# An encoder layer: two column blocks by feature half behind each sublayer, and another place for three small pieces of work

## The chip, the core and the metric

The kernel runs on one core of one Trainium2 chip. TensorE (PE) multiplies matrices, VectorE (DVE), ScalarE (ACT) and GpSimd (POOL) work on tiles in on-chip memory, and SyncE (SP) issues the DMA transfers. The metric is the device time of one execution in microseconds (us); lower is better.

## What is computed

One layer of an encoder on 256 tokens of 2048 features, in float32:

```python
f = _swiglu(_rmsnorm(h, ffn1_pre_g[i]), ffn1_w_gate[i], ffn1_w_up[i], ffn1_w_down[i])
h = h + 0.5 * _rmsnorm(f, ffn1_post_g[i])
m = _mixer(_rmsnorm(h, mix_pre_g[i]), w_qkv[i], na_rpb[i], out_g[i], w_o[i])
h = h + _rmsnorm(m, mix_post_g[i])
f = _swiglu(_rmsnorm(h, ffn2_pre_g[i]), ffn2_w_gate[i], ffn2_w_up[i], ffn2_w_down[i])
h = h + 0.5 * _rmsnorm(f, ffn2_post_g[i])
g = jax.nn.sigmoid(_rmsnorm(h, ple_pre_g[i]) @ w_ple_gate[i])
h = h + _rmsnorm(g * (p[i] @ w_ple_proj[i]), ple_post_g[i])
```

`_swiglu(u, wg, wu, wd)` is `(silu(u @ wg) * (u @ wu)) @ wd` with 5632 hidden features; `_mixer` projects to q, k and v for 16 heads of 128 features, attends (4 heads over a two-dimensional neighbourhood, 12 over dilated windows) and projects back with `w_o`. The last step adds a small input embedding `p`. `_rmsnorm` divides by the root of the mean square over the features and multiplies by a gain.

## The kernel before

**Tiles.** Tokens form two tiles `t` of 128; features are cut into slices `k` of 128 (16 of them) and into column blocks of 512, four slices each. `h`, the residual, stays on chip, tokens on partitions. For a product the left side must lie transposed, features on partitions: `transposed_split` (L238) turns four slices of a tile by TensorE (`tr`, L242, two banks), multiplies by the row gain (`y_g`, L246) and splits the result in a rounded part `u_h` (L248, ScalarE) and the rest `u_l` (L249, VectorE).

**Products.** A float32 product is made of three products of shorter precision: `mac` (L91, L92, L93) issues wh·u_h, wh·u_l and wl·u_h for each slice. A weight tile is loaded by SP (`raw`, L65, three buffers of 1 MB), rounded by ScalarE (`wh`, L73) and subtracted by VectorE (`wl`, L74). `product` (L101) runs over the slices in steps of eight, within a step over both token tiles, and can call `mid` before the last three slices of the last step. `pair_product` (L137) makes a gate block and an up block together from fewer products, with sums of token tiles made by `token_sums` (L252 to L267: `y_s` on VectorE, `sums_h` on ScalarE, `sums_l` on VectorE). Column block 0 of each feed-forward sublayer goes through `product` instead, gate first, then up.

**Start.** `load_x` (L292) fetches x transposed, two slices at a time (`xb`), and makes `u_h` (L300) and `u_l` (L301) with the row gain. The first gate block takes 1, 1, 2, 2, ... slices a step, so that work starts early. x·gain for the token sums is L373; the sums follow in the text of the program, and then the up block, four slices a step.

**Behind each sublayer.** The last down blocks are added to `f` (L401), their squares summed by ScalarE (`sq`, L235), and `f` multiplied by the gain in place (L404). `rsqrt_mean` (L223) makes the token's factor: a reduce on VectorE (L228) and two steps on POOL (L229, L230). `residual` (L320) then computes `h` (L332) block by block, and transposes it for the next sublayer. It is a generator, advanced at `mid` and after it, the first two column blocks of both tiles ahead of the last two. The next product starts as soon as the first `u_h` is there.

**Order.** The program is written for a framework that fixes the order of instructions on each engine when it is built, by its own estimates, and takes buffers from pools in turn. Each engine works through its own list in order; an instruction that waits holds all behind it on that engine.

Of the kernel before, what the change touches and what calls it, by code (L numbers as in the profile page):

```python
# [15 lines left out]
P = 128  # L16
# [17 lines left out]
def encoder_layer(ctx: ExitStack, tc: tile.TileContext, a: dict, out: bass.AP):  # L34
# [21 lines left out]
    make_identity(nc, ident)  # L56
    mhalf = const.tile([P, 16], F32, name="mhalf")
    nc.gpsimd.memset(mhalf, -0.5)


    def load_rows(w, r0, n, c0, pool=wpool, bufs=3):
# [39 lines left out]
    def product(  # L101
        acc, lhs, w, r0, c0, first=True, last=True, steps=None, ahead=None, mid=None, jobs=True
    ):

        nk = len(lhs)
        s0 = 0
        for n in steps or [nk % SUPER] * (nk % SUPER > 0) + [SUPER] * (nk // SUPER):
            if ahead is not None:
                ahead(s0)
            parts = load_parts(w, r0 + s0 * P, n, c0)
            for t in range(NT):
                xs = of_tile(lhs[s0 : s0 + n], t)
                lead, tail = first and s0 == 0, last and s0 + n == nk
                cut = n - MID if mid is not None and t == NT - 1 and s0 + n == nk else 0  # L120
                if cut > 0:
                    mac(acc[t], xs[:cut], parts[:cut], first=lead)
                    lead = False
                if mid is not None and t == NT - 1 and s0 + n == nk:
                    mid()
                cut = max(cut, 0)
                mac(acc[t], xs[cut:], parts[cut:], first=lead, last=tail)
            s0 += n
            if jobs:
                run_later()  # L130

    def run_later():
        for job in later:
            job()
        later.clear()
# [178 lines left out]
    def prenorm_factor(t):  # L314
# [2 lines left out]
            squares(h[:, t, b * NB : (b + 1) * NB], ss[:, b : b + 1])  # L317
        return rsqrt_mean(ss, D, 1.0)

    def residual(fg, ssf, scale, blocks, rs, g, sums=None):  # L320

        blocks += [new_split(acts, "u", D // NB) for _ in range(D // NB)]
        r, y0 = [], []
        for b0 in range(0, D // NB, 2):
            for t in range(NT):
                if b0 == 0:
                    r.append(rsqrt_mean(ssf[t], D, scale))
                for b in range(b0, b0 + 2):  # L330
                    cols = slice(b * NB, (b + 1) * NB)
                    nc.vector.scalar_tensor_tensor(  # L332
                        h[:, t, cols], fg[:, t, cols], r[t], h[:, t, cols], op0=ALU.mult, op1=ALU.add
                    )
# [14 lines left out]
    def swiglu(pool, f, ssf, res, blocks, rs, sums, w_gate, w_up, w_down, g_post):  # L349
        lhs = rows(blocks)  # L350
        ffn_pool[0] = pool
        f0 = 0

        def gated(x, t):
            y = pool.tile([P, NB], F32, name="gs", bufs=3)
            nc.scalar.activation(y, x, AF.Silu, scale=rs[t])
            return y

        for gi, ng in enumerate(FF_GROUPS):
            hid = []  # L360
            for nb in range(f0, f0 + ng):
                c0 = nb * NB
                if nb > 0:
                    gate, up = pair_product(lhs, sums, w_gate, c0, w_up, c0)
                    gs = [gated(gate[t], t) for t in range(NT)]
                else:
                    gate, up = accs("gate"), accs("up")
                    if rs is None:
                        steps = [1, 1] + [2] * 7
                        product(gate, lhs, w_gate, 0, c0, steps=steps, ahead=load_x)  # L370
                        for i, x in enumerate(x_first):
                            g = row_g[:, 0, 2 * i : 2 * i + 2].unsqueeze(2).broadcast_to([P, 2, S])
                            nc.vector.tensor_tensor(x, x, g, op=ALU.mult)  # L373
                        a1, a2 = x_first
                        half = [slice(t * P, (t + 1) * P) for t in range(NT)]
                        sums += token_sums(*(x[:, :, h_] for h_ in half for x in (a1, a2)))
                        product(up, lhs, w_up, 0, c0, steps=[4] * 4, ahead=load_h)
                        rs = [prenorm_factor(t) for t in range(NT)]
                        gs = [gated(gate[t], t) for t in range(NT)]
                    else:  # L380
                        product(gate, lhs, w_gate, 0, c0)
                        gs = [gated(gate[t], t) for t in range(NT)]
                        product(up, lhs, w_up, 0, c0)
                split_ = new_split(pool, "hid", 3)
                for t in range(NT):
                    y = up[t] if nb > 0 else pool.tile([P, NB], F32, name="hm", tag="part", bufs=6)
                    nc.vector.scalar_tensor_tensor(y, up[t], rs[t], gs[t], op0=ALU.mult, op1=ALU.mult)
                    later.append(lambda y=y, s_=split_, t=t: transposed_split(y, *s_, t))
                hid.append(split_)
            last = gi == len(FF_GROUPS) - 1  # L390
            hrows = rows(hid)
            for b in range(D // NB):
                gp = gain(g_post, b * NB, "g_post") if last else None
                acc = accs("down")

                def down_out(t):
                    f_t = f[:, t, b * NB : (b + 1) * NB]
                    if gi == 0:
                        nc.scalar.copy(f_t, acc[t])
                    else:  # L400
                        nc.vector.tensor_tensor(f_t, f_t, acc[t], op=ALU.add)  # L401
                    if last:
                        squares(f_t, ssf[t][:, b : b + 1])
                        nc.vector.tensor_tensor(f_t, f_t, gp, op=ALU.mult)  # L404

                def mid():
                    down_out(0)
                    if last and b == D // NB - 1:
                        next(res)

                product(acc, hrows, w_down, f0 * NB, b * NB, steps=[KB] * ng if b == 0 else None, mid=mid)
                down_out(1)
            f0 += ng
# [16 lines left out]
    with ExitStack() as att:  # L430
# [124 lines left out]
        for g in range(4):  # L555
            if g == 0:
                c = (0, w_na, 2 * w_na)
            else:
                c = tuple(3 * w_na + i * w_dil + (g - 1) * NB for i in range(3))
            acc = accs("q")  # L560
            product(acc, lhs, a["w_qkv"], 0, c[0])
            qT = heads_transposed(acc, rq, g > 0, "qT")
            acc = accs("k")
            product(acc, lhs, a["w_qkv"], 0, c[1])
            kT = heads_transposed(acc, rs, g > 0, "kT")
            acc = accs("v")
# [80 lines left out]
    for b in range(D // NB):  # L647
        cols = slice(b * NB, (b + 1) * NB)
        gp = gain(a["ple_post_g"], b * NB, "g_post")
        acc = accs("pg")  # L650
        product(acc, lhs, a["w_ple_gate"], 0, b * NB)
        for t in range(NT):
            s = pool.tile([P, NB], F32, name="sig", bufs=2)
            nc.scalar.activation(s, acc[t], AF.Sigmoid, scale=rs[t])
            nc.vector.tensor_tensor(s, s, pp[b * NT + t], op=ALU.mult)
            squares(s, ssz[t][:, b : b + 1])
            nc.vector.tensor_tensor(z[:, t, cols], s, gp, op=ALU.mult)
# [79 lines left out]
```

## Time and profile before

| | us |
|---|---|
| three runs | 1965.56, 1967.81, 1968.16 |
| their median | 1967.81 |
| the profiled execution | 1969.06 |
| its span in the profile | 1967.0 |
| TensorE busy in it | 1941.9 |
| VectorE busy | 1340.8 |
| ScalarE busy | 994.5 |

The profiled execution is one run more, taken with a hardware profiler; its span goes from the first to the last recorded instruction. In its timeline the stages stand so: first feed-forward sublayer 0 to 722 us, mixer to 1131, second feed-forward sublayer to 1848, the input embedding's projections and gate to 1957, and the last sums and stores to 1967. Rows of a timeline give the start, the duration, engine, line, operation, output<-inputs and, in brackets, the idle time before it and what ended it. Two matmuls that follow each other directly start 0.227 us apart, although each takes 0.39: they overlap.

### The profile page before, as it was taken

To read this page: it belongs to the slowest core of one execution; us is meant where nothing else is said; L and a number is where in the kernel's file an instruction comes from. 1 tells how busy PE (TensorE), PEld (TensorE's weight loads), DVE (VectorE), ACT (ScalarE), POOL (GpSimd) and SP (SyncE) were. 2 spreads that over 40 slices of the span, in tenths; PEclk is the share of its full clock that TensorE was granted. 3 is DMA by queue.
4 is the path that set the end of the run, shared out by engine and by line. 5 is a ranking of instruction groups with operands and counts; after the bars stand their busy time and mean duration, and the time that the engine had idled before them with its cause. 6 is when DMAs were issued, how large, how long until landed. Compare 5 with 4: busy or idle time off the path is not lost.

```text
span 1967.0 us, 22833 instructions
## 1 busy us (share of the span) xinstructions
PE 1941.9 (99%) x8840; PEld 1607.5 (82%) x8840; DVE 1340.8 (68%) x1484; ACT 994.5 (51%) x1215; POOL 28.3 (1%) x47
## 2 busy tenths in 40 slices
PE   8999999999999999999999999999999999999997
PEld 6888888888888878888888878888888888888886
DVE  5874787578757776566665588747865786577764
ACT  6554555345534545544545465545543554354563
POOL 0000000000000000000000000000000000000000
PEclk9999999999999999999999999999999999999999
DMA  9665556555655556454454665655565557555563
GB/s 336 211 214 192 193 184 219 187 180 193 214 192 174 174 176 230 141 191 152 151 192 143 215 203 193 216 191 176 188 233 173 193 172 235 171 193 177 170 216 111
DMA packets 190348, 376.91 MB, mean 192 GB/s; under 512 B 6432, under 2 KB 9504, under 8 KB 189984
## 3 DMA queue, kind: packets, MB, share of 16 engines
q1 hardware_dynamic: 190240, 375.46, 56.8%
q8 instruction: 69, 1.13, 0.2%
q14 instruction: 39, 0.32, 0.0%
HBM read 373.33 MB, written 2.10 MB: 191 GB/s over the span
## 4 chain that ended last, share of the span: by engine, by line
PE 96%; DVE 2%; DMA 1%; ACT 0%; issue 0%; POOL 0%; SPq 0%; DVEq 0%; POOLq 0%; ACTq 0%
PE down L91 8%; PE down L93 8%; PE down L92 8%; PE pair_z L93 3%; PE pair_x L91 3%; PE pair_y L91 3%; PE pair_z L92 3%; PE pair_x L92 3%; PE pair_y L92 3%; PE pair_z L91 3%; PE pair_x L93 3%; PE pair_y L93 3%; PE pair_v L92 3%; PE pair_v L91 3%; PE pair_v L93 3%; PE pair_s L92 2%
## 5 line engine op out<-in xcount | busy, mean ns | idle before, releaser
L74 DVE TENSOR_TENSOR wl<-raw,wh 128x1024 fp32r<-128x1024 f32 (+1 forms) x753 | 910.4, 1220 | 447.4 <-ACT wh L73 419.1
L73 ACT CAST wh<-raw 128x1024 fp32r<-128x1024 f32 (+1 forms) x753 | 790.1, 1052 | 728.5 <-PE pair_z L92 178.5
L91 PE MATMUL down<-wh,hid_h 128*128 128x512 f32 x704 | 274.7, 391 | 0.2
L93 PE MATMUL down<-wl,hid_h 128*128 128x512 f32 x704 | 274.1, 389 | 0.0
L92 PE MATMUL down<-wh,hid_l 128*128 128x512 f32 x704 | 273.9, 389 | 0.0
L91 PEld LDWEIGHTS down<-wh,hid_h 128*128 128x128 f32 x704 | 132.2, 188 | 28.1 <-ACT hid_h L248 1.1
L93 PEld LDWEIGHTS down<-wl,hid_h 128*128 128x128 f32 x704 | 132.2, 188 | 27.4
L92 PEld LDWEIGHTS down<-wh,hid_l 128*128 128x128 f32 x704 | 132.2, 188 | 27.1
L91 PE MATMUL pair_y<-wh,u_h 128*128 128x512 f32 x280 | 108.9, 389 | 0.0
L92 PE MATMUL pair_y<-wh,u_l 128*128 128x512 f32 x280 | 108.9, 389 | 0.0
L93 PE MATMUL pair_y<-wl,u_h 128*128 128x512 f32 x280 | 108.9, 389 | 0.0
L91 PE MATMUL pair_x<-wh,u_h 128*128 128x512 f32 x280 | 108.9, 389 | 0.0
L92 PE MATMUL pair_x<-wh,u_l 128*128 128x512 f32 x280 | 108.9, 389 | 0.0
L93 PE MATMUL pair_x<-wl,u_h 128*128 128x512 f32 x280 | 108.9, 389 | 0.0
L164 DVE TENSOR_TENSOR raw<-raw 128x1024 f32<-128x1024 f32 x80 | 97.7, 1221 | 1.4
L93 PE MATMUL pair_z<-wl,u_h 128*128 128x512 f32 x240 | 93.4, 389 | 0.0
L91 PE MATMUL pair_v<-wh,u_h 128*128 128x512 f32 x240 | 93.4, 389 | 0.0
L92 PE MATMUL pair_v<-wh,u_l 128*128 128x512 f32 x240 | 93.4, 389 | 0.0
L93 PE MATMUL pair_v<-wl,u_h 128*128 128x512 f32 x240 | 93.4, 389 | 0.0
L91 PE MATMUL pair_z<-wh,u_h 128*128 128x512 f32 x240 | 93.4, 389 | 0.0
L92 PE MATMUL pair_z<-wh,u_l 128*128 128x512 f32 x240 | 93.4, 389 | 0.0
L401 DVE TENSOR_TENSOR f<-f,down 128x512 f32<-128x512 f32 x48 | 32.8, 683 | 44.4 <-PE down L93 44.4
(199 smaller groups left out, 3117.9 us busy)
## 6 DMA issues: line engine op xcount, KB each, us to landing
raw<-in_ffn_w_up SPq DMA_DIRECT2D x88, 1024.0 KB, 5.1
raw<-in_ffn_w_down SPq DMA_DIRECT2D x88, 1024.0 KB, 4.9
raw<-in_ffn_w_gate SPq DMA_DIRECT2D x84, 1024.0 KB, 5.1
raw<-in_w_qkv SPq DMA_DIRECT2D x48, 1024.0 KB, 5.1
raw<-in_w_o SPq DMA_DIRECT2D x16, 1024.0 KB, 5.0
raw<-in_w_ple_gate SPq DMA_DIRECT2D x16, 1024.0 KB, 5.2
raw<-in_ffn_w_gate SPq DMA_DIRECT2D x7, 512.0 KB, 5.7
xb<-in_xT SPq DMA_DIRECT2D x8, 256.0 KB, 5.3
```

Of the source, the lines that this page charges most:

```text
L73: nc.scalar.copy(wh[:, :n], raw)
L74: nc.vector.tensor_tensor(wl[:, :n], raw, wh[:, :n].bitcast(F32), op=ALU.subtract)
L91: nc.tensor.matmul(acc, xh, wh, start=lead, stop=False)
L92: nc.tensor.matmul(acc, xl, wh, start=False, stop=False)
L93: nc.tensor.matmul(acc, xh, wl, start=False, stop=tail)
L164: nc.vector.tensor_tensor(out_, x, y, op=ALU.add)
L401: nc.vector.tensor_tensor(f_t, f_t, acc[t], op=ALU.add)
```

## The change

Four pieces. (1) A tiny activation, `warm`, reads `mhalf` right after that is set, so the table of functions is loaded for it. (2) `halves` takes two column blocks together: the first eight slices of block a, then of block b, then the second eight of each. It is used for gate and up of the second feed-forward sublayer's first block, for q and k of the mixer's first group of heads, and for the first two gate blocks of the input embedding. (3) In the first feed-forward sublayer, the token sums are written behind the up product, and are not to be issued ahead of the latest weight load. (4) The last column block of `f`, times its gain, goes to a tile of its own, `fg`.

```diff
+    nc.scalar.activation(small.tile([P, 1], F32, name="warm"), mhalf[:, :1], AF.Copy, scale=mhalf[:, :1])
...
+    def halves(lhs, a_, b_):
+        n = len(lhs) // 2
+        for r0 in (0, n):
+            for acc, w, c0 in (a_, b_):
+                product(acc, lhs[r0 : r0 + n], w, r0 * P, c0, first=r0 == 0, last=r0 > 0)
...
+    last_f = {}
+
     def residual(fg, ssf, scale, blocks, rs, g, sums=None):
...
+                    fg_t = last_f.pop(t) if b == D // NB - 1 and t in last_f else fg[:, t, cols]
                     nc.vector.scalar_tensor_tensor(
-                        h[:, t, cols], fg[:, t, cols], r[t], h[:, t, cols], op0=ALU.mult, op1=ALU.add
+                        h[:, t, cols], fg_t, r[t], h[:, t, cols], op0=ALU.mult, op1=ALU.add
                     )
...
                         product(gate, lhs, w_gate, 0, c0, steps=steps, ahead=load_x)
-                        for i, x in enumerate(x_first):
-                            g = row_g[:, 0, 2 * i : 2 * i + 2].unsqueeze(2).broadcast_to([P, 2, S])
-                            nc.vector.tensor_tensor(x, x, g, op=ALU.mult)
-                        a1, a2 = x_first
-                        half = [slice(t * P, (t + 1) * P) for t in range(NT)]
-                        sums += token_sums(*(x[:, :, h_] for h_ in half for x in (a1, a2)))
                         product(up, lhs, w_up, 0, c0, steps=[4] * 4, ahead=load_h)
+                        with tc.issue_after(raw_loads[-1].ins):
+                            for i, x in enumerate(x_first):
+                                g = row_g[:, 0, 2 * i : 2 * i + 2].unsqueeze(2).broadcast_to([P, 2, S])
+                                nc.vector.tensor_tensor(x, x, g, op=ALU.mult)
+                            a1, a2 = x_first
+                            half = [slice(t * P, (t + 1) * P) for t in range(NT)]
+                            sums += token_sums(*(x[:, :, h_] for h_ in half for x in (a1, a2)))
...
                     else:
-                        product(gate, lhs, w_gate, 0, c0)
+                        halves(lhs, (gate, w_gate, c0), (up, w_up, c0))
                         gs = [gated(gate[t], t) for t in range(NT)]
-                        product(up, lhs, w_up, 0, c0)
...
                         squares(f_t, ssf[t][:, b : b + 1])
-                        nc.vector.tensor_tensor(f_t, f_t, gp, op=ALU.mult)
+                        fg = f_t
+                        if b == D // NB - 1:
+                            fg = last_f[t] = pool.tile([P, NB], F32, name="fg", tag="gs", bufs=3)
+                        nc.vector.tensor_tensor(fg, f_t, gp, op=ALU.mult)
...
-            acc = accs("q")
-            product(acc, lhs, a["w_qkv"], 0, c[0])
-            qT = heads_transposed(acc, rq, g > 0, "qT")
-            acc = accs("k")
-            product(acc, lhs, a["w_qkv"], 0, c[1])
-            kT = heads_transposed(acc, rs, g > 0, "kT")
+            if g == 0:
+                acc, acc_k = accs("q"), accs("k")
+                halves(lhs, (acc, a["w_qkv"], c[0]), (acc_k, a["w_qkv"], c[1]))
+                qT = heads_transposed(acc, rq, g > 0, "qT")
+                kT = heads_transposed(acc_k, rs, g > 0, "kT")
+            else:
...
-        acc = accs("pg")
-        product(acc, lhs, a["w_ple_gate"], 0, b * NB)
+        if b < 2:
+            if b == 0:
+                pg = [accs("pg"), accs("pg")]
+                halves(lhs, *((pg[i], a["w_ple_gate"], i * NB) for i in range(2)))
+            acc = pg[b]
+        else:
...
```

**At the start, on ScalarE.** The first instructions of its list before (line, operation, output<-inputs, size, and how often in a row):

```order
L300 ACT_TABLE_LOAD
L300 ACTIVATE u_h<-xb,row_g 128x256 x2
L73 CAST wh<-raw 128x512 x2
L300 ACTIVATE u_h<-xb,row_g 128x256 x2
L73 CAST wh<-raw 128x1024
L300 ACTIVATE u_h<-xb,row_g 128x256 x4
L263 CAST sums_h<-y_s 128x512
L73 CAST wh<-raw 128x1024
L263 CAST sums_h<-y_s 128x512
```

And after the change, where the line numbers of the file have grown (L75 is the cast of L73, L310 is L300, L273 is L263):

```order
L60 ACT_TABLE_LOAD
L60 ACTIVATE warm<-mhalf 128x1
L310 ACTIVATE u_h<-xb,row_g 128x256 x2
L75 CAST wh<-raw 128x512 x2
L310 ACTIVATE u_h<-xb,row_g 128x256 x2
L75 CAST wh<-raw 128x1024
L310 ACTIVATE u_h<-xb,row_g 128x256 x2
L75 CAST wh<-raw 128x1024
L310 ACTIVATE u_h<-xb,row_g 128x256 x2
L273 CAST sums_h<-y_s 128x512
L75 CAST wh<-raw 128x1024
L273 CAST sums_h<-y_s 128x512
```

The table load stands ahead of everything that needs x, and one more weight cast stands ahead of the first cast of the token sums. Both casts of the sums are still among the gate steps.

**At the start, on SP.** The transfers issued first, before:

```order
L65 DMA raw<-in_ffn_w_gate 128x512 x2
L297 DMA xb<-in_xT 128x2x256
L65 DMA raw<-in_ffn_w_gate 128x2x512
L297 DMA xb<-in_xT 128x2x256 x2
L65 DMA raw<-in_ffn_w_gate 128x4x512
L65 DMA raw<-in_ffn_w_gate 128x2x512 x2
```

and after (L67 is the weight load, L307 the load of x):

```order
L67 DMA raw<-in_ffn_w_gate 128x512 x2
L307 DMA xb<-in_xT 128x2x256
L67 DMA raw<-in_ffn_w_gate 128x2x512
L307 DMA xb<-in_xT 128x2x256
L67 DMA raw<-in_ffn_w_gate 128x2x512
L307 DMA xb<-in_xT 128x2x256
L67 DMA raw<-in_ffn_w_gate 128x2x512 x2
```

The 1 MB tile (128x4x512), gate rows for the first `pair_product`, is gone from this place; it now stands behind the fourth load of `up`. The first 1 MB load of `up` in turn now stands ahead of the last piece of x.

**Between the first feed-forward sublayer and the mixer, on VectorE.** From the last `down` block of token tile 0 (`down_5289`) on, before; `down_5290` is that of tile 1:

```order
L401 TENSOR_TENSOR f<-f,down_5289 128x512
L404 TENSOR_TENSOR f<-f,g_post 128x512
L228 TENSOR_REDUCE m<-ssf 128x1
L74 TENSOR_TENSOR wl<-raw,wh 128x1024
L332 SCALAR_TENSOR_TENSOR h<-f,r,h 128x512 x3
L246 TENSOR_TENSOR y_g<-tr,row_g 128x512 x2
L401 TENSOR_TENSOR f<-f,down_5290 128x512
L332 SCALAR_TENSOR_TENSOR h<-f,r,h 128x512
L249 TENSOR_TENSOR u_l<-y_g,u_h 128x4x128 x2
```

And after, with the same blocks named `down_5291` and `down_5292`:

```order
L414 TENSOR_TENSOR f<-f,down_5291 128x512
L420 TENSOR_TENSOR fg<-f,g_post 128x512
L238 TENSOR_REDUCE m<-ssf 128x1
L345 SCALAR_TENSOR_TENSOR h<-f,r,h 128x512 x3
L345 SCALAR_TENSOR_TENSOR h<-fg,r,h 128x512
L256 TENSOR_TENSOR y_g<-tr,row_g 128x512 x2
L76 TENSOR_TENSOR wl<-raw,wh 128x1024
L259 TENSOR_TENSOR u_l<-y_g,u_h 128x4x128 x2
L414 TENSOR_TENSOR f<-f,down_5292 128x512
```

The weight remainder `wl` moved from behind the reduce to behind `y_g`; the fourth `h` stands ahead of `y_g`, and tile 1's `f` behind `u_l`. On TensorE, in the same place, 23 instead of 15 matmuls of `q` stand ahead of tile 1's first transposes.

**Between the second feed-forward sublayer and the input embedding, on TensorE.** The projections `pp` are 48 matmuls. At their end, before:

```order
L91 MATMUL pp_14028<-wh,p_h 128x512
L92 MATMUL pp_14028<-wh,p_l 128x512
L93 MATMUL pp_14028<-wl,p_h 128x512
L242 MATMUL tr<-ident,h 128x128 x8
L91 MATMUL pg_14122<-wh,u_h 128x512
```

and after, in the middle of the 48:

```order
L93 MATMUL pp_13986<-wh,p_h 128x512
L94 MATMUL pp_13986<-wh,p_l 128x512
L95 MATMUL pp_13986<-wl,p_h 128x512
L252 MATMUL tr<-ident,h 128x128 x16
L93 MATMUL pp_14009<-wh,p_h 128x512
```

The first transposes of token tile 1 moved from behind the last `pp` matmul to the middle, with sixteen in a row where there were eight. Eight more stand behind the last `pp`, ahead of the first `pg`.

More of the change, by code (lines that the diff above doesn't have):

```diff
@@ L559, in encoder_layer @@
                 c = tuple(3 * w_na + i * w_dil + (g - 1) * NB for i in range(3))
-            acc = accs("q")
-            product(acc, lhs, a["w_qkv"], 0, c[0])
-            qT = heads_transposed(acc, rq, g > 0, "qT")
-            acc = accs("k")
-            product(acc, lhs, a["w_qkv"], 0, c[1])
-            kT = heads_transposed(acc, rs, g > 0, "kT")
+            if g == 0:
[4 more added lines that the diff above has]
+            else:
+                acc = accs("q")
+                product(acc, lhs, a["w_qkv"], 0, c[0])
+                qT = heads_transposed(acc, rq, g > 0, "qT")
+                acc = accs("k")
+                product(acc, lhs, a["w_qkv"], 0, c[1])
+                kT = heads_transposed(acc, rs, g > 0, "kT")
             acc = accs("v")
@@ L649, in encoder_layer @@
         gp = gain(a["ple_post_g"], b * NB, "g_post")
-        acc = accs("pg")
-        product(acc, lhs, a["w_ple_gate"], 0, b * NB)
+        if b < 2:
[4 more added lines that the diff above has]
+        else:
+            acc = accs("pg")
+            product(acc, lhs, a["w_ple_gate"], 0, b * NB)
         for t in range(NT):
```

## Prediction

> **What bounds the kernel now.** I read the page's share of each engine first, then its chain of work that ended last.
>
> ```profile
> PE 1941.9 (99%) x8840; PEld 1607.5 (82%) x8840; DVE 1340.8 (68%) x1484; ACT 994.5 (51%) x1215; POOL 28.3 (1%) x47
> PE 96%; DVE 2%; DMA 1%; ACT 0%; issue 0%; POOL 0%; SPq 0%; DVEq 0%; POOLq 0%; ACTq 0%
> ```
>
> TensorE is busy for 99% of the span and is 96% of the chain. The change neither adds nor removes a TensorE instruction, so only time in which TensorE stands still, or runs at half clock, can move. Next, therefore, the table of stretches (length, then busy time of PE, PEld, DVE, ACT and POOL with counts, granted clock, DMA share, GB/s).
>
> ```profile
> 0.00:40.00 40.00, 31.16 (x118) 24.57 (x119) 25.01 (x38) 24.28 (x41) 0.97 (x9) 0.96 0.90 320
> 40.00:722.00 682.00, 681.89 (x3053) 565.23 (x3053) 479.51 (x477) 342.96 (x377) 1.26 (x3) 1.00 0.59 198
> 722.00:760.00 38.00, 34.27 (x162) 26.74 (x161) 31.81 (x46) 22.45 (x41) 6.57 (x8) 1.00 0.55 182
> 1125.00:1145.00 20.00, 18.50 (x90) 14.29 (x90) 14.86 (x24) 7.88 (x13) 2.40 (x4) 1.00 0.44 152
> 1845.00:1880.00 35.00, 33.99 (x166) 27.91 (x165) 29.86 (x42) 21.35 (x35) 2.81 (x4) 1.00 0.63 218
> ```
>
> The stretches left out are as full as the second row. The idle time lies in four places, which are the four that the change touches: the start (40.00 − 31.16 = 8.8 us), the hand-off from the first feed-forward sublayer to the mixer (3.7), from the mixer to the second (1.5), and from that to the input embedding (1.0). That is 15 us in all, plus what the start loses at half clock. No change here can bring more than about 17 us, and the realistic part is smaller. The waits of TensorE say who is waited for (us in total, times, longest):
>
> ```profile
> PE gate L91 <- ACT wh L73: 8.8, 2, 7.0
> PE q L91 <- ACT u_h L248: 1.5, 1, 1.5
> PE q L93 <- DVE wl L74: 1.0, 1, 1.0
> PE gate L92 <- DVE u_l L249: 0.9, 1, 0.9
> ```
>
> **The start.** The timeline (start, duration) shows the table load first, then a stall, then the end of the first `gate` product.
>
> ```profile
> 0.86 0.11 POOL L58 MEMSET mhalf<- 128x16 f32 x1
> ...
> 4.22 1.28 ACT L300 ACT_TABLE_LOAD   x1 [4.22 <-DMA xb<-in_xT]
> 6.99 0.79 PE L91 MATMUL gate<-wh,u_h 128*128 128x512 f32 x1 [6.99 <-ACT wh L73]
> ...
> 15.04 0.62 ACT L263 CAST sums_h<-y_s 128x512 fp32r<-128x512 f32 x1 [3.00 <-DVE y_s L259]
> 15.57 1.04 ACT L73 CAST wh<-raw 128x1024 fp32r<-128x1024 f32 x1
> 16.66 0.50 PE L91 MATMUL gate<-wh,u_h 128*128 128x512 f32 x1 [1.79 <-ACT wh L73]
> ...
> 34.60 0.39 PE L92 MATMUL gate<-wh,u_l 128*128 128x512 f32 x1
> 34.83 0.39 PE L93 MATMUL gate<-wl,u_h 128*128 128x512 f32 x1
> ```
>
> The load of the function table stands behind the first piece of x, for 1.28 us. In the new order the tiny activation on `mhalf` stands ahead; `mhalf` is written at 0.86, so the load is done before x arrives. The first matmul comes at 6.99 − 1.28, about 5.7. This term, −1.3, is the surest of all.
>
> Then ScalarE waits 3.00 us for the token sums' `y_s`, with weight casts queued behind; TensorE goes idle for 1.79 us, and this is what follows, in consecutive stretches:
>
> ```profile
> 11.50:14.90 3.40, 3.37 (x15) 2.44 (x13) 3.37 (x9) 0.55 (x2) 0.00 (x0) 1.00 1.05 400
> 14.90:18.30 3.40, 1.57 (x6) 1.01 (x7) 2.88 (x5) 3.26 (x5) 0.00 (x0) 1.00 0.77 282
> 18.30:21.70 3.40, 3.40 (x10) 2.62 (x9) 3.40 (x6) 2.46 (x6) 0.00 (x0) 0.50 0.68 172
> 728.23:731.65 3.42, 1.95 (x11) 1.19 (x9) 3.42 (x7) 1.95 (x3) 0.00 (x0) 1.00 0.00 0
> 731.65:735.06 3.41, 3.09 (x14) 2.41 (x14) 2.84 (x5) 0.76 (x3) 1.53 (x2) 1.00 0.17 33
> ```
>
> A stretch of 3.40 us with TensorE busy for 1.57 (46%) is followed by one at clock 0.50, which loses half of itself, about 1.65 us. A stretch with 1.95 of 3.42 (57%) is not followed by one. The stall thus costs 1.79 + 1.65, plus small waits around it: 3.5 to 3.9 us.
>
> How much of that goes? By its words, the change writes the sums behind `up`. The built order says otherwise: the sums still stand early on VectorE and ScalarE, among the gate steps, though spread out, one weight cast and one activation further back. And the 1 MB load for the first pair of blocks, which stood on SP between the small gate loads, now stands behind the last `up` load. I follow that order by hand with the durations of the rows above (cast 1.04, sums 0.62). Without the 1 MB, at the 400 GB/s of the first of these stretches 2.6 us of transfer, the weights of the third to fifth gate steps land 2 to 3 us earlier; their casts end near 11.4, 13.9 and 16.7 instead of 16.6 and later; the wait for `y_s` falls behind a cast whose matmuls still feed TensorE. So the 1.79 and the 1.65 go. What is late next is x itself: its last piece now stands behind a 1 MB load of `up`, its `u_l` is ready near 29.4, and twelve matmuls at 0.227 (start to start, 34.60 to 34.83 as in any dense run of rows) hang on it. The last gate matmul lands near 31.5 instead of 34.83, with three `up` matmuls (0.7) already done. The start gives 34.83 − 31.5 + 0.7 = **−4.0 us**. Bounds: −1.3 if the stall stays whole, −5.2 if all goes (1.3 + 3.9).
>
> [...]
>
> **First feed-forward sublayer to mixer.** The chain from the last `down` block of token tile 0 to the first `q` matmul:
>
> ```profile
> 723.58 0.63 ACT L235 ACTIVATE sq<-f 128x512 f32<-128x512 f32 x1 [4.04 <-DVE f L401]
> 724.34 0.69 DVE L404 TENSOR_TENSOR f<-f,g_post 128x512 f32<-128x512 f32 x1 [0.85 <-ACT sq L235]
> 725.28 1.23 DVE L74 TENSOR_TENSOR wl<-raw,wh 128x1024 fp32r<-128x1024 f32 x1 [0.18 <-ACT wh L73]
> 725.46 1.45 POOL L230 TENSOR_TENSOR r<-m,mhalf 128x1 f32<-128x1 f32 x1
> 726.95 2.08 DVE L332 SCALAR_TENSOR_TENSOR h<-f,r,h 128x512 f32<-128x512 f32 x3 [0.44 <-POOL r L230]
> ...
> 730.14 0.67 DVE L401 TENSOR_TENSOR f<-f,down 128x512 f32<-128x512 f32 x1
> 731.32 0.50 PE L91 MATMUL q<-wh,u_h 128*128 128x512 f32 x1 [1.48 <-ACT u_h L248]
> 731.40 1.28 DVE L249 TENSOR_TENSOR u_l<-y_g,u_h 128x512 fp32r<-128x512 f32 x2
> 734.62 0.55 POOL L230 TENSOR_TENSOR r<-m,mhalf 128x1 f32<-128x1 f32 x1
> 735.20 2.08 DVE L332 SCALAR_TENSOR_TENSOR h<-f,r,h 128x512 f32<-128x512 f32 x3 [0.72 <-POOL r L230]
> 751.45 0.50 PE L93 MATMUL q<-wl,u_h 128*128 128x512 f32 x1 [1.00 <-DVE wl L74]
> ```
>
> What gains: `fg` doesn't overwrite what the squares read, so the multiply no longer waits 0.85 and the reduce behind it starts 0.6 earlier. No `wl` stands behind that reduce, and POOL's `r`, which took 1.45 beside a `wl` and 0.55 at 734.62, gives 0.9. Tile 0's `h` starts 1.5 earlier. What is given back: the fourth `h` (2.08 / 3 = 0.69) now stands ahead of `y_g`, so the first matmul of `q` comes only 0.8 earlier; a `wl` of 1.2 stands ahead of `u_l`; and tile 1's `f` stands behind that `wl` and both `u_l`, not ahead of the `u_l`, near 731.75 instead of 730.14. On an unchanged chain from there (735.20 − 730.14 = 5.1), tile 1's `h` starts near 736.8 instead of 735.20, 1.6 later. Its transposes stand eight matmuls further back on TensorE (8 × 0.227 = 1.8), reached 1.0 later with the 0.8 lead; TensorE waits there about 1.2, and about 0.85 for a transpose bank in the next group, which must be emptied first. The 1.00 for `wl` at 751.45 is covered: the halves of `q` and `k` together are 96 matmuls (22 us) on the first eight k's twice over, and VectorE catches up. With those gains and waits the 97th matmul of the projection comes within 0.1 us of where it did: nothing gained. Both heads' transposes now fall into the third block, `v`, where two banks serve them: the nearest row is the bank wait just worked out, 0.85, of which I count 0.7. Sum **+0.6 us**. Bounds: −3.7, if TensorE waits nowhere in this stretch (38.00 − 34.27), and +2.5, if none of the earlier start is kept (0.8) and a bank wait comes a second time (0.85).
>
> **Mixer to second feed-forward sublayer.** Here the rows around the hand-off are the same but for halves of `gate` and `up` in turn; the 0.9 for `u_l` lies at the first matmuls, ahead of where the halves differ: **0**, between −1.5 (its whole idle time) and +0.5.
>
> **Second feed-forward sublayer to input embedding.** Here the projections `pp`, which need nothing of `h`, cover the chain.
>
> ```profile
> 1851.41 1.45 POOL L230 TENSOR_TENSOR r<-m,mhalf 128x1 f32<-128x1 f32 x1
> ...
> 1855.62 0.39 PE L91 MATMUL pp<-wh,p_h 128*128 128x512 f32 x1
> ...
> 1860.58 3.40 DVE L332 SCALAR_TENSOR_TENSOR h<-f,r,h 128x512 f32<-128x512 f32 x5 [0.72 <-POOL r L230]
> 1866.52 1.03 PE L242 MATMUL tr<-ident,h 128*128 128x128 f32 x8
> 1869.18 0.66 PE L242 MATMUL tr<-ident,h 128*128 128x128 f32 x4 [0.46 <-DVE y_g L246]
> ```
>
> Before, tile 1's transposes stand behind all 48 `pp` matmuls (1855.6 to 1866.5), four microseconds after their `h`: nothing waits. After, sixteen stand between the 24th and the 25th `pp`. Tile 0 is 1.5 earlier, as in the first hand-off, but tile 1's `h` comes near where it did, 1860.6, while TensorE is at the middle of `pp` near 1860. By hand TensorE waits 1.4 for the first `h`, then 0.25 and 0.85 for banks and 0.2 more: 2.7. Against that stand 1.0 us of waits of before, which mostly go, and the rest of `pp` still lies behind to cover what follows. The 24th `pg` matmul comes near 1876.7 instead of 1875.2: **+1.5 us**. Bounds: −1.0, all waits of before gone, and +2.7, none of them gone. Halves of `pg` don't help, since `u` of the second half isn't waited for before either. The tail behind the last `pg` is unchanged.
>
> **Sum.** −4.0 + 0.6 + 0 + 1.5 = −1.9 us. The profiled execution took 1969.06 us (span 1967.0); by it the time would be 1967.2. It lies 1.25 above the median of the three runs, 1967.81, so I forecast 1967.81 − 1.9 = **1965.9 us**, no difference by 0.2% (3.9 us, about what a measurement of this kernel can tell from no change).
>
> **The rivals.**
> *All waits at the hand-offs go.* If VectorE keeps up with the new order, the waits of 1.48, 1.00 and the small ones at the first transposes fall away, 2.8 us, and at the embedding 0.9. For it: tile 0 is ready 1.5 earlier at both. Against: tile 1 stands later in the order at the first. With the start, −4.0 − 2.8 − 0.9 = −7.7: 1960.1. Chance 0.27, with a part that stops between.
> *The change doesn't do what it says.* The sums still stand early; if ScalarE's wait for `y_s` stalls TensorE as now, only the table load is saved: −1.3 + 0.6 + 1.5 = +0.8, 1968.6. For it: the order. Against: the load that lay ahead is gone. Chance 0.20.
> *Half clock at three places (slower).* A wait that leaves TensorE busy for less than half of a 3.4 us stretch is paid again with 1.65. It decides between 46% (closed) and 57% (open). At the first hand-off 1.95 of 3.42 is busy now; 0.4 us more of waiting closes it. At the embedding 2.7 us of waits, if they fall in one stretch, leave far less. With the start's stall kept (−1.3), the upper bound at the mixer and two such stretches: −1.3 + 2.5 + 1.5 + 3.3 = +6.0, 1973.8. Against: the new waits lie apart, with matmuls between them. [...] Chance 0.08; one stretch alone adds 1.65 to the forecast and stays inside no difference.
> The forecast has the other 0.45.
>
> **How the numbers follow.** The forecast's own range is 1963 to 1969, and a tenth of it lies under 1963.9. Faster by over 0.2%: 0.27 + 0.05 = 0.32; slower: 0.08; within: 0.60. The range that leaves out the far ends of the first and third rivals is 1961 to 1970.5.
>
> **What would show it.** The first matmul near 5.7; no stretch at clock 0.50 between 18 and 22 us; the last gate matmul near 31.5. At the mixer, a wait of `tr` for `h` of about 1 us and none for `wl` near 751; at the embedding, `tr` waiting for `h` in the middle of `pp`. The prediction is wrong if the start gives under 2 or over 5 us, or if the transposes of tile 1 wait nowhere.

## The result and the profile after

| | before | after |
|---|---|---|
| median of the runs, us | 1967.96 | 1981.07 |
| lowest and highest | 1965.56, 1968.16 | 1980.46, 1982.06 |
| span of the profiled execution | 1967.0 | 1980.0 |

The kernel takes 1.007 of the time of before, 95% interval 1.0058 to 1.0083, 13.1 us. I had forecast 1965.9 us, no difference, and a range up to 1970.5.

The page of the changed kernel, its busy times and the groups of the `down` product (busy, then mean ns of one):

```profile
PE 1956.1 (99%) x8840; PEld 1607.8 (81%) x8840; DVE 1340.6 (68%) x1484; ACT 994.1 (50%) x1216; POOL 26.5 (1%) x47
...
L93 PE MATMUL down<-wh,hid_h 128*128 128x512 f32 x704 | 278.5, 396 | 0.2
L94 PE MATMUL down<-wh,hid_l 128*128 128x512 f32 x704 | 277.8, 395 | 0.0
L95 PE MATMUL down<-wl,hid_h 128*128 128x512 f32 x704 | 277.7, 395 | 0.0
...
L93 PE MATMUL pair_y<-wh,u_h 128*128 128x512 f32 x280 | 108.9, 389 | 0.0
```

TensorE is busy 14 us longer with the same 8840 instructions (1941.9 before). It doesn't wait more; its instructions take longer, and not all of them: `pair_y` keeps the 389 ns it had, while `down` takes 396, 395 and 395. The same groups on the page of before:

```profile
L91 PE MATMUL down<-wh,hid_h 128*128 128x512 f32 x704 | 274.7, 391 | 0.2
L93 PE MATMUL down<-wl,hid_h 128*128 128x512 f32 x704 | 274.1, 389 | 0.0
L92 PE MATMUL down<-wh,hid_l 128*128 128x512 f32 x704 | 273.9, 389 | 0.0
```

The difference of 5 or 6 ns is easily passed over; times 2112 it is 12 us. In the timelines it shows as the distance between starts, here in an undisturbed stretch of the first feed-forward sublayer, first before, then after:

```profile
199.35 0.39 PE L93 MATMUL down<-wl,hid_h 128*128 128x512 f32 x1
...
200.71 0.39 PE L93 MATMUL down<-wl,hid_h 128*128 128x512 f32 x1
```

```profile
199.44 0.40 PE L95 MATMUL down<-wl,hid_h 128*128 128x512 f32 x1
...
200.84 0.40 PE L95 MATMUL down<-wl,hid_h 128*128 128x512 f32 x1
```

From one row to the other it is six starts: 1.36 / 6 = 0.227 us before, 1.40 / 6 = 0.233 after. Over all starts that follow each other by less than 0.4 us the means are 0.2274 and 0.2329 for `down`, 0.2299 and 0.2356 for the mixer's output product `mo`. So 2112 x 0.0055 = 11.6 us and 384 x 0.0057 = 2.2 us, 13.8 together; what is left for all I had reckoned with is about -0.7.

Each product of two tiles is two instructions here: a weight load (`LDWEIGHTS`, engine PEld, 128x128, for `down` 188 ns on average before), which takes the left side, and the matmul (128x512, 389 to 391 ns), which reads a tile of `wh` or `wl`. The expectations below call the left side the stationary operand and the `wh` or `wl` the moving one. Both slow products load `hid` as their left side. The other products with `wh` and `wl` load `u`, the token sums or `p`. What the change does to `hid` is not in any line about it: `warm` is a new tile in the pool `small`, four buffers of 32 bytes, and the pools opened later start 128 bytes further on. In the built programs, `hid` starts at byte 151040 of each partition before (590 x 256) and at 151168 after; `u`, `wh` and `wl` stay at multiples of 256.

The rest of the profile, against the steps. The start (first matmul, clock after it, waits):

```profile
5.53 0.80 PE L93 MATMUL gate<-wh,u_h 128*128 128x512 f32 x1 [5.53 <-ACT wh L75]
...
25.99 0.50 PE L94 MATMUL gate<-wh,u_l 128*128 128x512 f32 x1 [0.59 <-DVE u_l L311]
...
30.07 0.73 PE L93 MATMUL gate<-wh,u_h 128*128 128x512 f32 x2 [1.29 <-ACT u_h L310]
```

```profile
14.90:18.30 3.40, 3.40 (x17) 2.82 (x16) 3.25 (x5) 2.69 (x5) 0.00 (x0) 1.00 0.99 308
18.30:21.70 3.40, 3.40 (x17) 2.82 (x16) 3.11 (x6) 2.11 (x4) 0.00 (x0) 1.00 0.89 277
```

The table load has gone from the path, the stall and the half clock behind it too; in their place stand waits for the last pieces of x, 0.59 and 1.29. At the first hand-off, the last `down` of before and then the rows of after:

```profile
729.44 0.40 PE L93 MATMUL down<-wl,hid_h 128*128 128x512 f32 x1
```

```profile
728.74 0.55 POOL L240 TENSOR_TENSOR r<-m,mhalf 128x1 f32<-128x1 f32 x1
729.33 2.07 DVE L345 SCALAR_TENSOR_TENSOR h<-f,r,h 128x512 f32<-128x512 f32 x3 [0.95 <-POOL r L240]
...
733.22 0.40 PE L95 MATMUL down<-wl,hid_h 128*128 128x512 f32 x1
733.68 0.50 PE L93 MATMUL q<-wh,u_h 128*128 128x512 f32 x1
...
739.85 2.08 DVE L345 SCALAR_TENSOR_TENSOR h<-f,r,h 128x512 f32<-128x512 f32 x3 [0.72 <-POOL r L240]
740.71 0.63 PE L252 MATMUL tr<-ident,h 128*128 128x128 f32 x4 [0.35 <-issue]
...
742.59 0.66 PE L252 MATMUL tr<-ident,h 128*128 128x128 f32 x4 [0.55 <-DVE y_g L256]
```

`q` starts 0.46 behind the last `down`, 1.88 before (729.44 to 731.32). And in the middle of `pp`, where I had put the waits of the input embedding:

```profile
1872.78 1.29 PE L252 MATMUL tr<-ident,h 128*128 128x128 f32 x8 [0.55 <-DVE h L345]
1874.61 1.26 PE L252 MATMUL tr<-ident,h 128*128 128x128 f32 x8 [0.55 <-DVE y_g L256]
1876.48 0.50 PE L93 MATMUL pp<-wh,p_h 128*128 128x512 f32 x1 [0.62 <-ACT pp L660]
```

### The profile page after: what moved, and what is told of

It is laid out like the page before. It is cut to its first block, busy times and chain, and to the rows that moved or that the text cites. A ratio compares the mean times of both kernels' runs of the same rounds, so it can differ in the third digit from the quotient of the medians.

```text
span 1980.0 us, 22837 instructions
## 1 busy us (share of the span) xinstructions
PE 1956.1 (99%) x8840; PEld 1607.8 (81%) x8840; DVE 1340.6 (68%) x1484; ACT 994.1 (50%) x1216; POOL 26.5 (1%) x47
## 4 chain that ended last, share of the span: by engine, by line
PE 95%; DVE 2%; DMA 1%; ACT 1%; issue 0%; POOL 0%; SPq 0%; DVEq 0%; POOLq 0%; ACTq 0%
PE down L93 8%; PE down L94 8%; PE down L95 8%; PE pair_z L95 3%; PE pair_x L95 3%; PE pair_x L93 3%; PE pair_y L93 3%; PE pair_z L93 3%; PE pair_z L94 3%; PE pair_y L94 3%; PE pair_x L94 3%; PE pair_y L95 3%; PE pair_v L93 3%; PE pair_v L94 3%; PE pair_v L95 3%; PE pair_s L93 2%
## 5 line engine op out<-in xcount | busy, mean ns | idle before, releaser
L75 ACT CAST wh<-raw 128x1024 fp32r<-128x1024 f32 (+1 forms) x753 | 789.2, 1051 | 746.5 <-PE down L94 182.1
## 6 DMA issues: line engine op xcount, KB each, us to landing
xb<-in_xT SPq DMA_DIRECT2D x8, 256.0 KB, 4.9
```

The source lines that it names most:

```text
L75: nc.scalar.copy(wh[:, :n], raw)
```

## The experiments: is it the place of a tile?

Theory A: the 128 bytes. Rival B: the new order, or the longer program. Four kernels; the first is the kernel before with this line behind the `memset` of `mhalf`:

```diff
+    nc.gpsimd.memset(small.tile([P, 1], F32, name="pad"), 0.0)
```

> The kernel before with one change: a tile of one number per partition is taken from the pool of small tiles (four buffers of 32 bytes) and set once, so that every tile of the pools opened later, the hidden tiles of the feed-forward sublayers among them, lies 128 bytes further on, at 151168 instead of 151040; order and work stay as before. Theory A, the place of the hidden tiles in memory slows the matmuls that load them: down goes from 0.227 to 0.233 us a matmul, 2112 x 0.0057 = 12 us, and the mixer's output product 384 x 0.0057 = 2.2 us, so 1982 us. Rival B, the new order of work (or the longer program) slows down: the time stays at 1968 within 1.5 us and down at 0.227.

The other three are the changed kernel with another place for the output of the activation:

```diff
-    nc.scalar.activation(small.tile([P, 1], F32, name="warm"), mhalf[:, :1], AF.Copy, scale=mhalf[:, :1])
+    nc.scalar.activation(mhalf[:, 8:9], mhalf[:, :1], AF.Copy, scale=mhalf[:, :1])
```

> The changed kernel with one difference: the activation that loads the table writes into an unused column of mhalf instead of a new tile, so all tiles lie where they lay before; the order is that of the change. Theory A: down is back at 0.227 a matmul and the time falls by about 14 us, to 1967 (1965 to 1969). Rival B: it stays at 1981.

```diff
-    nc.scalar.activation(small.tile([P, 1], F32, name="warm"), mhalf[:, :1], AF.Copy, scale=mhalf[:, :1])
+    nc.scalar.activation(small.tile([P, 32], F32, name="warm")[:, :1], mhalf[:, :1], AF.Copy, scale=mhalf[:, :1])
```

> The changed kernel with the new small tile 32 numbers wide, so that the later tiles lie 512 bytes further on, and not 128. Theory A in the form that the hidden tiles must start at a multiple of 512 bytes: as with no shift, 1967. Theory A in the form that any other place (relative to the weights, say) is worse: 1981. Rival B: 1981.

The fourth has 16 in the place of 32.

> The changed kernel with the new small tile 16 numbers wide, so that the later tiles lie 256 bytes further on. If a multiple of 256 bytes is enough: 1967, down at 0.227. If 512 is needed: 1975 to 1981, down above 0.229. Rival B: 1981.

| | median, us | against before (interval) | `down`, us from start to start |
|---|---|---|---|
| before with 128 bytes more (e1) | 1980.59 | 1.0065 (1.0050 to 1.0080) | 0.2330 |
| change, no tile (e2) | 1967.64 | 1.0000 (0.9991 to 1.0009) | 0.2273 |
| change, 512 bytes (e3) | 1967.56 | 0.9999 (0.9990 to 1.0008) | 0.2273 |
| change, 256 bytes (e4) | 1966.75 | 0.9996 (0.9986 to 1.0005) | 0.2273 |

The first group of `down` on the page of e1, then on that of e2 (busy, then mean ns of one), shows the same:

```profile
L92 PE MATMUL down<-wh,hid_h 128*128 128x512 f32 x704 | 278.6, 396 | 0.2
```

```profile
L93 PE MATMUL down<-wh,hid_h 128*128 128x512 f32 x704 | 274.7, 391 | 0.2
```

The line that does nothing costs the kernel before 13 us; the whole change, without the shift, costs nothing and brings nothing that can be measured. Rival B falls. A shift of 256 or of 512 bytes is as good as none: 0.2273 in both.

**Which tile, and beside which?** Three kernels are the one before with one kind of operand moved, each taken from tiles that are 256 bytes larger. For `hid`, which with `bufs == 3` is that of the feed-forward sublayers and not the mixer's (in the `u` kernel the condition is `name == "u"`):

```diff
     def new_split(pool, name, bufs):
+        if name == "hid" and bufs == 3:
+            pad = [
+                pool.tile([P, KB * S + 64], F32R, name=f"{name}_{x}", tag=f"{name}_{x}", bufs=bufs)
+                for x in "hl"
+            ]
+            return tuple(x[:, 32 : 32 + KB * S].rearrange("p (k s) -> p k s", k=KB) for x in pad)
```

> The kernel before, with only the hidden tiles of the two feed-forward sublayers shifted: each is taken 256 bytes larger and used from byte 128 on, so every other tile keeps its place modulo 256 bytes; order and work as before. Theory A1, the stationary operand (the tile that is loaded into TensorE as weights) must start at a multiple of 256 bytes: down at 0.2325 us a matmul, mo at 0.230, 2112 x 0.0057 = +12 us, 1979.5. Rival A2, another of the tiles that moved (f, the sublayers' own raw, the parts of the pair products) was the cause: 1968.

> The kernel before, with only the u tiles (left side of gate, up, q, k, v, pg and of most of the pair products) used from byte 128 of tiles that are 256 bytes larger. Theory A1: some 5160 matmuls that load u go from 0.2267 to 0.2325, +29 us, 1997, while down stays at 0.2274. Rival A3, only the hidden tiles or their place relative to the weights matter: 1968.

```diff
-        wl = wpool.tile([P, 2, NB], F32R, name="wl", bufs=6)
+        wl = wpool.tile([P, 2 * NB + 64], F32R, name="wl", bufs=6)
+        wl = wl[:, 32 : 32 + 2 * NB].rearrange("p (k n) -> p k n", k=2)
```

> The kernel before, with only wl, the moving operand of a third of the matmuls, used from byte 128 of tiles that are 256 bytes larger. Theory A1 (only the stationary operand matters): 1968 within 1.5 us. Rival A4, whatever TensorE reads must be so aligned: some 2770 matmuls x 0.0057 = +16 us, 1984.

`hid` alone (e5): 1980.02 us (1.0062, 1.0046 to 1.0077). `u` alone (e6): 1998.60 (1.0157, 1.0139 to 1.0176). `wl` alone (e7): 2018.75 (1.0260, 1.0246 to 1.0274). The pages and the summaries of single tiles show the slow group move with the tile. For `hid` shifted, from the page (busy, mean ns of one):

```profile
L91 PE MATMUL down<-wh,hid_h 128*128 128x512 f32 x704 | 278.5, 396 | 0.2
...
L91 PE MATMUL pair_y<-wh,u_h 128*128 128x512 f32 x280 | 108.9, 389 | 0.0
```

For `u` shifted, from the summaries (minimum, median and maximum ns of one):

```profile
L91 PE MATMUL down<-wh,hid_h x704: 389/389/497, 145.0 to 1881.9; 128*128 128x512 f32 x176
...
L91 PE MATMUL pair_y<-wh,u_h x280: 390/394/404, 75.9 to 1832.7; 128*128 128x512 f32 x140
```

and for `wl` shifted:

```profile
L92 PE MATMUL pair_y<-wh,u_h x280: 392/392/393, 76.1 to 1852.0; 128*128 128x512 f32 x140
L93 PE MATMUL pair_y<-wh,u_l x280: 397/397/398, 76.3 to 1852.3; 128*128 128x512 f32 x140
L94 PE MATMUL pair_y<-wl,u_h x280: 395/395/395, 76.6 to 1852.5; 128*128 128x512 f32 x140
```

With `hid` or `u` off, the products that load it are slow and the others not; `mo`, whose `hid` wasn't moved, keeps 0.2299. But my form A1, that only the left side matters, falls with `wl`: it cost 51 us, not nothing, and not the 16 of a third of the matmuls either. All three steps of each slice are slow there, those two also that read nothing that was moved (392 and 397 ns on average in `pair_y`, 389 before). So here matmuls became slower by an operand that their neighbours read.

What is left is either that each operand must lie at a multiple of 256, or that those which TensorE reads close together must lie alike. One line ahead of all other tiles moves them all:

```diff
+    nc.gpsimd.memset(const.tile([P, 32], F32, name="pad"), 0.0)
     ident = const.tile([P, P], F32, name="ident")
```

> The kernel before, with 128 bytes taken and set once ahead of all other tiles, so that every operand of TensorE in the large products (u, sums, hid, wh, wl) starts 128 bytes behind a multiple of 256. The shift of hid cost 13 us, of u 31, of wl alone 51, although only a third of the matmuls read wl. Theory A5, each operand must start at a multiple of 256 bytes: the costs come together, 2020 us or more. Rival A6, the two operands that TensorE reads at a time must start alike modulo 256 bytes: here they do, 1968 within 2 us.

This kernel (e9) takes 1967.83 us (1.0002, 0.9992 to 1.0012), and the summary of its tiles:

```profile
L92 PE MATMUL down<-wh,hid_h x704: 388/389/497, 141.4 to 1852.7; 128*128 128x512 f32 x176
...
L92 PE MATMUL pair_y<-wh,u_h x280: 388/389/390, 73.8 to 1803.7; 128*128 128x512 f32 x140
```

Every operand of the large products lies 128 bytes off, and nothing is slower: 0.5 us against before, where 128 bytes on `hid` alone cost 12.8, on `u` alone 31.3 and on `wl` alone 51.5. What counts in these runs is not where a tile starts, but where the tiles start against each other modulo 256 bytes, that is, whether their start bytes leave the same remainder when divided by 256: with `hid` or `u` moved, the left side against `wh` and `wl`; with `wl` moved, `wl` against the left side, and against `wh` too. Two smaller steps of the shift, 64 bytes with two buffers instead of four and 32 bytes with `bufs=1`:

```diff
+    nc.gpsimd.memset(small.tile([P, 1], F32, name="pad", bufs=2), 0.0)
```

> The kernel before, with the extra small tile in two buffers instead of four, so that hid and what follows lies 64 bytes further on. If the step is 256 bytes: slower about as with 128, 1978 to 1982. If 64 bytes are enough: 1967.5, down at 0.2274.

> The kernel before with hid and what follows 32 bytes further on (one buffer of the extra small tile). If any place but a multiple of 256 bytes costs: 1979 to 1984. If the cost goes by how far apart the operands lie, with 64 bytes the worst: between 1968 and 1979.

64 bytes (e10): 1983.86 us (1.0079, 1.0066 to 1.0093); 32 bytes (e14): 1984.05 (1.0084, 1.0066 to 1.0102), `down` at 0.2339 in both. All three steps cost, the two smaller ones somewhat more than 128 bytes: 16.5 and 16.8 us against 13.2.

## The experiments: the parts of the change

With the shift out of the way, the parts can be read, from profiled executions: the start by the first `pair_s` matmul, the embedding by the time from the second sublayer's first `gate` to the last matmul.

Without `fg`, that is, with the gain multiplied in place again:

```diff
-                        fg = f_t
-                        if b == D // NB - 1:
-                            fg = last_f[t] = pool.tile([P, NB], F32, name="fg", tag="gs", bufs=3)
-                        nc.vector.tensor_tensor(fg, f_t, gp, op=ALU.mult)
+                        nc.vector.tensor_tensor(f_t, f_t, gp, op=ALU.mult)
```

> The changed kernel with the table load into a column of mhalf (no tile moved) and without fg: the last block is multiplied by its gain in place again. The transposes of token tile 1 then stand as before on TensorE, behind all 48 pp matmuls and behind 15 of q. My reading, that fg brings that order and that it costs about 2 us at the input embedding: the last matmul 2 us earlier than in the changed kernel without the shift, 1965.5. Rival, the halves of pg cost the 2 us: no earlier, 1967.5.

The median (e8) is 1966.21 us (0.9993, 0.9984 to 1.0002), inside the noise; the trace is clearer. From the second sublayer's first `gate` to the last matmul it takes 822.3 us, as before (822.3), against 824.2 in each of e2, e3 and e4. The wait of `tr` in the middle of `pp` comes with `fg`, not with the halves of `pg`, which stand in this kernel.

The activation into a column of `mhalf` alone, in the kernel before:

```diff
     nc.gpsimd.memset(mhalf, -0.5)
+    nc.scalar.activation(mhalf[:, 8:9], mhalf[:, :1], AF.Copy, scale=mhalf[:, :1])
```

> The kernel before with one line more, the activation into a column of mhalf; the token sums stay where they are written. Its order at the start is that of the changed kernel. My reading now, that this line alone moves the order at the start: first matmul 1.4 earlier, first pair product 3 to 3.8 earlier, 1964 to 1965. The reading of the prediction, that only the table load goes and the rest needs the sums' new place: first pair product 1.3 earlier, 1966.3.

This kernel (e11) takes 1965.90 us (0.9993, 0.9984 to 1.0001). Its first `pair_s` is at 55.05, 1.8 ahead of the first profile of before, between the two readings. But the order at the start is the new one, there is no stall at 14.5 and no half clock behind it (granted clock 1.00 from 10 to 60 us); a wait of 0.65 for weights and waits of 0.76 and 0.63 for pieces of x stand in their place. The order of the built programs settles the rest: the token sums written behind `up`, and nothing else, leave each engine's order as before, row for row; added to this one line, or taken out of e2, they change no row either. The move of the token sums does nothing; the one line moves the 1 MB load and the sums, presumably because the framework then estimates another time for the table load.

The best of the parts, `fg` in the first sublayer alone:

```diff
+        own_fg = rs is None
...
-                        if b == D // NB - 1:
+                        if b == D // NB - 1 and own_fg:
```

> The changed kernel with the table load into a column of mhalf, and fg in the first feed-forward sublayer alone; the transposes behind the second stand as before, behind all pp matmuls. From the parts as measured: start -3.5, first hand-off -0.8, embedding 0, so the last matmul 4.3 us earlier than in the kernel before and 1963 us; if the first hand-off gives nothing, 1964.

This kernel (e12) takes 1966.16 us (0.9990, 0.9981 to 0.9999), not 1963. From the second sublayer's first `gate` to the last matmul it takes 822.3, as expected; against the first profile of before, the start gave 3.05, and the first hand-off and the mixer 0.16 the wrong way. The same kernel with `ident` moved to a multiple of 256, to see whether transposes follow the rule:

```diff
+    nc.gpsimd.memset(const.tile([P, 32], F32, name="pad"), 0.0)
     ident = const.tile([P, P], F32, name="ident")
...
-    mhalf = const.tile([P, 16], F32, name="mhalf")
+    mhalf = const.tile([P, 48], F32, name="mhalf")
```

> The kernel of the run before (table load into a column of mhalf, fg in the first feed-forward sublayer alone) with ident moved by 128 bytes to a multiple of 256, and everything behind the constants by 256; order and work the same. In the transposes ident is the moving operand and h the stationary one; until now they lie 128 bytes apart modulo 256. If the rule of equal places holds for them too, the 370 or so transposes that follow each other start some 3 to 6 ns closer, 1 to 2 us less, 1964 to 1965. If it doesn't (they are matmuls of plain float32 and 128 columns): 0.098 us as before and 1966.

This kernel (e13) takes 1966.61 us (0.9994, 0.9985 to 1.0003), and the mean distance of transposes is 0.1003, 0.1002 without: no change that shows. Either transposes of 128 columns don't pay, or what they pay is hidden.

## Why the prediction was wrong

**The step that failed** is this sentence at the head of the working: "The change neither adds nor removes a TensorE instruction, so only time in which TensorE stands still, or runs at half clock, can move." The duration of the same instruction moved. I had costed `warm` by what it does, as "the surest of all", and not by the tile it takes; the place of tiles was in no term, no bound and no rival. e1 shows that such a tile alone adds 13 us to the kernel before, and e2 that without it the change is worth nothing measurable.

**The other terms**, read without the shift, missed by 0 to 1.5 us each.

| term | forecast, us | measured, us |
|---|---|---|
| start | -4.0 | -2.5 |
| first hand-off, with the mixer | +0.6 | 0.0 |
| second hand-off | 0 | 0 |
| input embedding | +1.5 | +1.9 |
| place of `hid` | none | +13.8 |

Without the last row they sum to -0.6; the medians of e2, e3 and e4 lie between 0.2 above and 0.7 below before.

*The start.* The first `pair_s` comes at 56.4 on average in the eight traces with the old order (55.1 to 57.2), and at 54.0 in the eight with the new one (53.0 to 55.0). The mechanism was right, the stall and half clock go, and x is late next, as forecast. The size was off, for two reasons. x is later than summed: in the changed kernel TensorE waits until 30.07 for the `u_h` of a late piece, where I had its `u_l` at 29.4, and the last gate matmul starts at 33.50, not near 31.5. And the profile I summed from was no average one, since the half clock shows in six of the eight old traces alone: from 18.3 to 21.7 us the granted clock is 0.50 in before, 0.52 to 0.72 in e5, e6, e7, e10 and e14, and 1.00 in e1 and e9. Whether it comes went with where the stall fell. In the trace of before the clock changes first at 11.50 us, where matmuls that started 0.43 us apart come to start 0.23 apart; it is at half from 18.33 to 21.74, and again from 1960.51. Behind the first change these three times lie 2, 3 and 571 times 3.4133 us. In the trace of after it changes at 9.47 and 1972.13, 575 times 3.4133 apart. Counted in such stretches from the first change of each trace, e9, where the clock stays full, and the first hand-off of e5, where it halves:

```profile
15.40:18.81 3.41, 2.08 (x8) 1.43 (x9) 2.93 (x5) 3.41 (x7) 0.00 (x0) 1.00 0.64 228
18.81:22.22 3.41, 3.41 (x17) 2.81 (x16) 3.41 (x6) 2.46 (x5) 0.00 (x0) 1.00 0.74 209
```

```profile
734.89:738.30 3.41, 1.63 (x8) 0.83 (x6) 3.41 (x7) 2.43 (x4) 0.00 (x0) 1.00 0.00 0
738.30:741.72 3.42, 3.40 (x8) 2.73 (x9) 2.70 (x5) 0.28 (x2) 1.64 (x2) 0.50 0.19 64
```

In before, the stretch ahead of the half clock (14.92 to 18.33) is busy for 1.60 of 3.41 us, and the one at the first hand-off (728.30 to 731.71), which is followed by clock 1.00, for 1.94. Of these four, 1.60 and 1.63 are followed by half clock, 1.94 and 2.08 are not. So the two edges of the prediction, 46% and 57%, hold in these traces. e9 stands idle from 14.90 to 18.30 for 1.80 us, almost as long as the 1.83 of before, but only 1.33 of it lies in the stretch from 15.40, and it stays free of half clock.

*The first hand-off.* `r` takes 0.55 (forecast 0.55), `q` starts 1.4 earlier (0.8), tile 1's `h` stands 6.63 behind the last `down` instead of 5.76, 0.9 later (1.6), and TensorE waits 0.35 and 0.55 at the transposes (1.2 for `h` and 0.85 for a bank; the profile names no releaser for the 0.35). Each has the sign I gave it, and together they give nothing: from the first `pair_s` to the second sublayer's first `gate` it takes 1077.4 on average in the five traces with this order and no tile shifted against another (e2, e3, e4, e12, e13: 1076.9 to 1077.8), and 1077.4 in the four without `fg` (before, e8, e9, e11: 1077.1 to 1077.7). Part of what eats the earlier `q` can be seen: from the first `v` matmul to the first `mo` it takes 256.0 to 256.1 in all seven traces with the halves of `q` and `k`, and 255.0 to 255.1 in the seven others in which neither `u` nor `wl` was moved alone, so 1.0 where I had counted 0.7. The wait for `wl` didn't go: in e2 it is 1.0 again, at a `k` matmul.

*The second hand-off.* e8, which has all the halves but not `fg`, takes as long as before from there to the end, 822.3.

*The embedding.* As forecast, in the place forecast: `tr` waits for `h`, then for a bank. That the halves of `pg` wouldn't help was right too; that `fg` brings the order was not known until e8.

**The rivals.** That the change doesn't do what it says was right for the token sums, but their price wasn't: the stall went all the same. The half clock at the hand-offs didn't come in the changed kernel: the granted clock is 1.00 in the stretches of both (722 to 760 and 1845 to 1880 us). It can come there without the change, though: e5 has the first hand-off's order of before, and shows a clock of 0.50 from 738.30 to 741.72.

## What to carry to other kernels

When an edit adds a tile, look where the tiles behind it come to lie, before and after; here 128 bytes in an early pool moved `hid` from 151040 to 151168, and the kernel took 13 us longer. If matmuls of one product get some per cent slower with no wait between them (`down` here: 0.2274 to 0.2329 us), compare the start addresses of left side and weights modulo 256 bytes, and give small tiles room in multiples of 256 or a spare column of a tile that is there: e4, e3 and e2 cost nothing that shows (0.9996, 0.9999 and 1.0000 of before). Sum a change against several executions where the stretch that it touches varies from one to the next.

## What the runs showed of the hardware

Float32 matmuls of 512 columns, three to a slice here, went from 0.227 us each to 0.233 or 0.234 when the left side and the weights came to start differently modulo 256 bytes within a partition (`down` in e1, e10 and e14). 256 and 512 bytes of shift cost nothing that shows (e4, e3), 32, 64 and 128 bytes 13 to 17 us on 2496 matmuls (e14, e10, e1), and 128 bytes on both sides nothing (e9). The weight loads themselves don't show it: their mean for `down` is 188 ns before, 188 and 189 after.

Where they start differently, the matmuls start 5 to 7 ns further apart on average (0.2274 to 0.2329 for `down` in after, 0.2339 in e10 and e14), with no more waiting between them: the idle time before the three groups of `down` is 0.2 us in all on the page of after, as on that of before. Why a neighbour's operand slows a matmul is not shown by these runs. Open too is why `wl` alone, which a third of the matmuls read, cost as much per slice (0.2300, 0.2357 and 0.2341 from start to start of the three `down` steps, against 0.2267) as a shift of all loads of `hid`.
